# Up projections of two gated FFNs as Strassen block products, between the halves of the gate projection

## Chip, cores and metric

The kernel runs on one core of a Trainium2 chip, in one launch. The metric is the device time of one execution in microseconds. The core has a matrix engine (TensorE, PE in the profile; PEld is its loading of weights), a vector engine (VectorE, DVE), an engine for activation functions and scaled copies (ScalarE, ACT), a general one (GpSimd, POOL) and one that issues most of the DMAs (SyncE, SP).

## What is computed

Two layers over 512 tokens of 1024 features, fp32. Each layer is a mixer and a gated FFN, both after an RMS norm and both added to the residual; a last RMS norm follows. The change concerns the FFNs, the same in both layers, with 2816 hidden features:

```python
def gated_conv_ffn(x, w_gate, w_up, conv_w, conv_b, w_down):
    g = jnp.einsum('bsd,df->bsf', x, w_gate)
    g = causal_dwconv3(g, conv_w) + conv_b
    up = jnp.einsum('bsd,df->bsf', x, w_up)
    return jnp.einsum('bsf,fd->bsd', jax.nn.silu(g) * up, w_down)
...
    hn = rms_norm(h, norm_ffn[layer])
    h = h + gated_conv_ffn(hn, w_ffn_gate[layer], w_ffn_up[layer], conv_ffn[layer],
                           b_conv_ffn[layer], w_ffn_down[layer])
return rms_norm(h, final_norm)
```

`causal_dwconv3` is a convolution of three taps along the tokens, for each feature by itself.

## The kernel before

**Layout.** Activations lie transposed: features on the 128 partitions, the 512 tokens along the columns. The residual is eight tiles `h[k]`. An FFN's 2816 hidden features are 22 tiles of 128, taken in pairs f, f+1.

**Precision.** Each fp32 operand is held as two parts: a high part, rounded to the matrix engine's format by a copy on ScalarE, and a low part, the rest, by a subtraction on VectorE. One product of two operands is then three matmuls into the same bank, high by high, high by low, low by high (`mm3`, L126 to L128). Weights come from HBM by SyncE's queue into `raw` (four buffers of 512 KB, `fetch`), and `parts` makes `whi` (L121, ScalarE) and `wlo` (L122, VectorE), five buffers each. The split activations are `hgh` and `hgl`.

**Norm.** `Norm.add` multiplies a finished tile of h by the norm's gain, splits it into `hg[k]`, and sums its squares into `ssq`. The division by the norm is left for later: `rstd` adds `ssq` over the partitions by two matmuls with ones (L184, L185) and makes 1/sqrt on ScalarE and VectorE (L201 to L211), once the first pair's gates are done. Where a per-token column is wanted instead, L193 does it with one-column matmuls.

**An FFN.** `gate_up` handles one pair: two gate tiles and two up tiles, four banks of 512 columns, eight k tiles, three matmuls each: 96 matmuls of 512 columns. As each gate bank ends, VectorE evicts it times rstd into a padded row buffer (L465), three taps of the convolution follow on VectorE (L231 to L233), silu on ScalarE (L469), and GpSimd multiplies by rstd (L470), which is the up tile's norm. As each up bank ends, VectorE multiplies it with that (L474) and `split` makes the activation's two parts (L221, L223). After six pairs (and again after the other five; `HALVES`) the down projection adds into h, in layer 0 by `project` (weights against activations, two groups of four banks), in layer 1 by `group8` with eight banks, tokens on partitions. In layer 1 the residual is transposed into `y` by `turn_residual` during pairs 2 to 8.

**Order.** Instructions go to each engine's queue in an order that the Tile framework fixes when the program is built, and each queue is worked off in order. An instruction waits until its operands are there and its buffer is free; the number of buffers of a tag (`bufs`) limits how far an engine runs ahead. Seven banks of PSUM belong to matmul groups, one to small things.

Of the kernel before, what the change touches and what calls it, by code (L numbers as in the profile page):

```python
# [8 lines left out]
F32 = mybir.dt.float32  # L9
# [21 lines left out]
def tile_trunk(ctx: ExitStack, tc: tile.TileContext, x, norm_mix, norm_ffn, final_norm,  # L31
# [85 lines left out]

    def parts(raw, a, b, name):
        hi = wp.tile([P, a, b], F32R, tag="whi", bufs=5, name=f"whi_{name}")
        lo = wp.tile([P, a, b], F32R, tag="wlo", bufs=5, name=f"wlo_{name}")  # L120
        nc.scalar.activation(hi, raw, AF.Copy)  # L121
        nc.vector.tensor_tensor(lo, raw, hi.bitcast(F32), ALU.subtract)  # L122
        return hi, lo
# [6 lines left out]
    def group(name, outs, ks, lhs, rhs, tail, on_done, before=None):  # L130
# [6 lines left out]
        for i, j in order:  # L137
# [6 lines left out]
            if i == len(ks) - 1:  # L144
                on_done(j, banks[j])


    h = [cp.tile([P, S], F32, name=f"h{k}") for k in range(NK)]
# [6 lines left out]
    class Norm:  # L155
# [22 lines left out]
        def rstd(self):  # L178
            ps = aux_bank(f"ss_{self.name}")
            hi = tp.tile([P, S], F32R, tag=f"ms{S}", bufs=1, name=f"ssh_{self.name}")  # L180
            lo = tp.tile([P, S], F32R, tag=f"sd{S}", bufs=1, name=f"ssl_{self.name}")
# [14 lines left out]

    def newton(ms, n, name, r):


        sd = tp.tile([P, max(n, LINE)], F32, tag=f"sd{max(n, LINE)}", bufs=1, name=f"sd_{name}")[:, :n]  # L200
# [5 lines left out]
    def inv_sqrt(r, ss, n, name):  # L206

        ms = tp.tile([P, max(n, LINE)], F32, tag=f"ms{max(n, LINE)}", bufs=1, name=f"ms_{name}")[:, :n]
# [226 lines left out]
    HALVES = ((0, 12), (12, 22))  # L435

    def gate_up(layer, prm, rstd, ap, acts, f, tail):

        cs = slice(f * P, (f + 2) * P)
        ch = {}  # L440
        for half in range(2):
            for key, w in (("g", w_ffn_gate), ("u", w_ffn_up)) if tail < NK else ():
                ch[key, half] = weights(w[layer][half * 512 : (half + 1) * 512, cs]
                                        .rearrange("(k p) c -> p k c", p=P), 4, 256,
                                        f"{key}{layer}_{f}_{half}")
        if tail == NK:
            for key, w in (("g", w_ffn_gate), ("u", w_ffn_up)):
                for half in range(2):
                    ch[key, half] = weights(w[layer][half * 512 : (half + 1) * 512, cs]
                                            .rearrange("(k p) c -> p k c", p=P), 4, 256,  # L450
                                            f"{key}{layer}_{f}_{half}")

        def lhs(k, j):
            hi, lo = ch["gu"[j // 2], k // 4]
            c = slice((j % 2) * P, (j % 2 + 1) * P)
            return hi[:, k % 4, c], lo[:, k % 4, c]

        gates = {}

        def done(j, ps):  # L460
            ft = f + j % 2
            r = rstd()
            if j < 2:
                t = padded_tile()
                nc.vector.tensor_tensor(t[:, 2:], ps, r, ALU.mult)  # L465
# [3 lines left out]
                nc.scalar.activation(s, c, AF.Silu, bias=prm("bf", ft))  # L469
                nc.gpsimd.tensor_tensor(s, s, r, ALU.mult)  # L470
                gates[j] = s
            else:
                s = gates[j - 2]
                nc.vector.tensor_tensor(s, ps, s, ALU.mult)  # L474
                acts[ft] = split(ap, s, f"a{layer}_{ft}", tag="a", bufs=12)

        group(f"gu{layer}_{f}", range(4), list(range(NK)), lhs, lambda k, j: hg_k(k), tail, done)

    def lazy_rstd(norm):
        got = []  # L480

        def get():
            if not got:
                got.append(norm.rstd())
            return got[0]

        return get

    def ffn0(norm):
        nonlocal prm1  # L490
        with tc.tile_pool(name="f0", bufs=1) as ap:
            rstd = lazy_rstd(norm)
            nxt = None
            for a, b in HALVES:
                acts = {}
                for f in range(a, b, 2):
                    gate_up(0, prm0, rstd, ap, acts, f, 4 if f == 0 else NK)
# [3 lines left out]
                project(f"d0_{a}", w_ffn_down[0], acts, list(range(a, b)), nxt)  # L501
# [127 lines left out]
    def ffn1(norm):  # L629
        with tc.tile_pool(name="f1", bufs=1) as ap:  # L630
            fin = ap.tile([P, D], F32, name="fin")
            nc.scalar.dma_start(fin, final_norm.rearrange("(o d) -> o d", o=1).to_broadcast([P, D]))
            rstd = lazy_rstd(norm)
# [3 lines left out]
            def turn_residual(t):  # L637
                for half in range(2):
                    ps = mm_bank(f"hT{t}_{half}")
                    for i in range(4):  # L640
                        nc.tensor.transpose(ps[:, i * P : (i + 1) * P],
                                            h[half * 4 + i][:, t * P : (t + 1) * P], ident)
                    nc.scalar.copy(y[t][:, half * 512 : (half + 1) * 512], ps)
# [100 lines left out]
```

## Time and profile before

| | before |
|---|---|
| median of 3 runs | 1023.85 us (1020.9 to 1025.29) |
| profiled execution, its own time | 1023.1 us |
| span of its profile | 1021.4 us |
| mean granted TensorE clock | 0.998 |
| PE busy, matmuls | 1009.4 us, 99% |
| PEld busy | 832.4 us, 81% |
| DVE busy | 559.0 us, 55% |
| ACT busy | 345.3 us, 34% |
| POOL busy | 126.7 us, 12% |
| DMA | 101.24 MB, 99 GB/s on the mean |

Busy times are sums over the engine's instructions. PE and PEld run side by side, so their shares don't add up. The span is the time from the first instruction to the last in the profile; the execution's own time is 1.7 us longer. In the groups of the profile, `gu<-hgh,whi_g` is an FFN matmul into a gate or up bank from the high part of h and the high part of a gate weight; `128*128 128x512` is its weight tile and its moving tile.

### The profile page before, as it was taken

What the parts mean: (1) busy time and instruction counts of PE and PEld (TensorE: products, weight loads), DVE (VectorE), ACT (ScalarE), POOL (GpSimd) and SP (SyncE); (2) the same over time, 40 slices, a digit from 0 to 9 for tenths busy, and PEclk for the clock granted to TensorE, in tenths of its full rate; (3) what the DMA queues carried; (4) which work ended last, traced back from release to release, by engine and by line L of the source; (5) the groups of instructions that cost most, each with busy time, mean ns of one, the idle gap of its engine ahead of it and who ended that gap; (6) DMA issues with size and microseconds to landing.
All of it is one profiled execution on the core that took longest, in us unless ns stands there. A gap on an engine that the chain in (4) does not pass through costs nothing.

```text
span 1021.4 us, 11177 instructions
## 1 busy us (share of the span) xinstructions
PE 1009.4 (99%) x4485; PEld 832.4 (81%) x4485; DVE 559.0 (55%) x706; ACT 345.3 (34%) x449; POOL 126.7 (12%) x113
## 2 busy tenths in 40 slices
PE   9999999999999999999999999999999999999997
PEld 6788888888888888888878888888888888888885
DVE  5997567755623455654423645486554226565526
ACT  5423443323312223333345444433332212332313
POOL 3141121111100011111110001211111001111100
PEclk9999999999999999999999999999999999999999
DMA  7432233332333332332333123324233224233302
GB/s 232 154 103 83 83 103 98 92 115 89 95 111 84 96 109 83 103 104 78 106 126 103 62 91 96 103 83 124 83 103 103 84 81 124 83 104 103 100 3 83
DMA packets 74719, 101.24 MB, mean 99 GB/s; under 512 B 3268, under 2 KB 52652, under 8 KB 74668
## 3 DMA queue, kind: packets, MB, share of 16 engines
q1 hardware_dynamic: 73324, 98.96, 31.2%
q10 hardware_dynamic: 1344, 1.58, 0.5%
q8 instruction: 35, 0.57, 0.2%
q14 instruction: 16, 0.13, 0.0%
HBM read 98.42 MB, written 2.10 MB: 98 GB/s over the span
## 4 chain that ended last, share of the span: by engine, by line
PE 97%; DVE 1%; DMA 1%; issue 0%; POOL 0%; ACT 0%; DVEq 0%; POOLq 0%; ACTq 0%
PE gu L127 16%; PE gu L128 16%; PE gu L126 16%; PE dn L127 4%; PE d L126 4%; PE d L128 4%; PE dn L128 4%; PE d L127 4%; PE dn L126 4%; PE oo L128 1%; PE u L127 1%; PE u L126 1%; PE oo L127 1%; PE u L128 1%; PE oe L127 1%; PE oe L126 1%
## 5 line engine op out<-in xcount | busy, mean ns | idle before, releaser
L126 PE MATMUL gu<-hgh,whi_g 128*128 128x512 f32 x352 | 137.3, 390 | 0.0
L128 PE MATMUL gu<-hgh,wlo_g 128*128 128x512 f32 x352 | 137.0, 389 | 0.0
L128 PE MATMUL gu<-hgh,wlo_u 128*128 128x512 f32 x352 | 137.0, 389 | 0.0
L127 PE MATMUL gu<-hgl,whi_g 128*128 128x512 f32 x352 | 136.9, 389 | 0.0
L126 PE MATMUL gu<-hgh,whi_u 128*128 128x512 f32 x352 | 136.9, 389 | 0.0
L127 PE MATMUL gu<-hgl,whi_u 128*128 128x512 f32 x352 | 136.9, 389 | 0.0
L470 POOL TENSOR_TENSOR s<-s,rstd_f 128x512 f32<-128x512 f32 x44 | 66.5, 1512 | 529.8 <-ACT s L469 529.8
L121 ACT ACTIVATE whi_g<-raw_g 128x1024 fp32r<-128x1024 f32 x44 | 46.6, 1059 | 169.9 <-PE gu L127 107.8
L122 DVE TENSOR_TENSOR wlo_u<-raw_u,whi_u 128x1024 fp32r<-128x1024 f32 x52 | 63.8, 1229 | 59.5 <-ACT whi_u L121 59.1
L122 DVE TENSOR_TENSOR wlo_g<-raw_g,whi_g 128x1024 fp32r<-128x1024 f32 x44 | 54.4, 1236 | 47.3 <-ACT whi_g L121 46.9
L126 PEld LDWEIGHTS gu<-hgh,whi_u 128*128 128x128 f32 x352 | 66.1, 188 | 13.8
L127 PEld LDWEIGHTS gu<-hgl,whi_u 128*128 128x128 f32 x352 | 66.1, 188 | 13.7
L128 PEld LDWEIGHTS gu<-hgh,wlo_g 128*128 128x128 f32 x352 | 66.1, 188 | 13.7
L126 PEld LDWEIGHTS gu<-hgh,whi_g 128*128 128x128 f32 x352 | 66.1, 188 | 13.6
L128 PEld LDWEIGHTS gu<-hgh,wlo_u 128*128 128x128 f32 x352 | 66.1, 188 | 13.6
L127 PEld LDWEIGHTS gu<-hgl,whi_g 128*128 128x128 f32 x352 | 66.1, 188 | 13.6
L121 ACT ACTIVATE whi_u<-raw_u 128x1024 fp32r<-128x1024 f32 x52 | 55.0, 1059 | 58.6 <-PE gu L127 20.7
L126 PE MATMUL d<-a_hi,whi_d 128*128 128x512 f32 x176 | 68.6, 390 | 0.0
L128 PE MATMUL d<-a_hi,wlo_d 128*128 128x512 f32 x176 | 68.5, 389 | 0.0
L127 PE MATMUL d<-a_lo,whi_d 128*128 128x512 f32 x176 | 68.5, 389 | 0.0
L126 PE MATMUL dn<-whi_dn,a_hi 128*128 128x512 f32 x176 | 68.5, 389 | 0.0
L127 PE MATMUL dn<-wlo_dn,a_hi 128*128 128x512 f32 x176 | 68.5, 389 | 0.0
(236 smaller groups left out, 1772.5 us busy)
## 6 DMA issues: line engine op xcount, KB each, us to landing
raw_g<-in_w_ffn_gate_dram SPq DMA_DIRECT2D x44, 512.0 KB
raw_u<-in_w_ffn_up_dram SPq DMA_DIRECT2D x44, 512.0 KB, 3.9
raw_d<-in_w_ffn_down_dram SPq DMA_DIRECT2D x22, 512.0 KB, 3.5
raw_dn<-in_w_ffn_down_dram SPq DMA_DIRECT2D x22, 512.0 KB, 3.3
raw_oe<-in_w_out_even_dram SPq DMA_DIRECT2D x8, 512.0 KB, 3.3
raw_v<-in_w_in_odd_dram SPq DMA_DIRECT2D x8, 512.0 KB, 3.6
raw_u<-in_w_in_odd_dram SPq DMA_DIRECT2D x8, 512.0 KB, 3.5
raw_oo<-in_w_out_odd_dram SPq DMA_DIRECT2D x8, 512.0 KB, 3.3
```

The source lines that it names most:

```text
L121: nc.scalar.activation(hi, raw, AF.Copy)
L122: nc.vector.tensor_tensor(lo, raw, hi.bitcast(F32), ALU.subtract)
L126: nc.tensor.matmul(ps, lhs[0], rhs[0], start=start, stop=False)
L127: nc.tensor.matmul(ps, lhs[0], rhs[1], start=False, stop=False)
L128: nc.tensor.matmul(ps, lhs[1], rhs[0], start=False, stop=stop)
L470: nc.gpsimd.tensor_tensor(s, s, r, ALU.mult)
```

## The change

Of the 11 pairs of an FFN the first two (f = 0 and 2) stay as they were, now in `Ffn.direct`. The other nine (`Ffn.seven`) compute the two up tiles as a product of 2 by 2 blocks. With A the two weight tiles against the two halves of the contraction, and B the normalized activations, the two halves of the contraction against the two halves of the tokens, it makes

- sums of weights S1 = A21+A22, S2 = S1-A11, S3 = A11-A21, S4 = A12-S2 (tiles `s14`, `s23`),
- sums of activations T1 = B12-B11, T3 = B22-B12, T2 = T3+B11, T4 = B21-T2 (tiles `t41`, `t23`), once in an FFN,
- seven block products P1 = A11 B11, P2 = A12 B21, P3 = S4 B22, P4 = A22 T4, P5 = S1 T1, P6 = S2 T2, P7 = S3 T3, each twelve matmuls (four k pairs, three parts) of 256 columns,
- the four blocks of the result P1+P2, P1+P6+P5+P3, P1+P6+P7+P4, P1+P6+P7+P5. P1, P6, P7 and P4 are accumulated in one bank, with copies of the bank kept between them.

So 48 matmuls of 512 columns become 84 of 256. On TensorE the order in such a pair is P1, the first half of the gates' k tiles, P6, the second half, P7, P5, P2, P4, P3.

What goes with it:

- The sums need activations that are normalized in full. During pair 2, `normalize` multiplies two h tiles at a time by gain and rstd, splits them into `hg` again, makes their four sums and splits those. In pairs from 4 on the gates are evicted without rstd, by a copy on ScalarE, and GpSimd's multiplication is gone.
- The first tap of the convolution moves from VectorE to ScalarE.
- In those pairs the gate weights' low part is no longer made by VectorE: `summed` copies the raw weights times -1 to `lo` on ScalarE, and a DMA issued from GpSimd's queue adds `raw` to it; `hi` is a second copy on ScalarE. (The copy to `lo` rounds to the matrix engine's format, so the sum is the rest that the subtraction gave.)
- The activations are projected down in four parts of an FFN (`PARTS`) instead of two, and `a` has 6 buffers instead of 12.
- In layer 1 the T2, T3 tiles take the buffers of the residual tiles h, so `turn_residual` moves into pair 0's loop over k, and pair 0's tail, the last k tiles that each bank goes through by itself, is two k tiles instead of four. The final norm's gain is loaded late, into a `raw` buffer. Some small tiles share buffers (`pk`, and the norm's work tiles in `sq`).

The diff, cut to its core (in the changed kernel the matmul of `multiply` is line 621, those of `mm3` are L135 to L137):

```diff
-        pk = cp.tile([P, P], F32, tag=f"pk{layer}", name=f"pk{layer}")
+        pk = cp.tile([P, P], F32, tag="pk", bufs=1, name=f"pk{layer}")
...
+    def summed(raw, a, b, name):
+
+        hi = wp.tile([P, a, b], F32R, tag="whi", bufs=5, name=f"whi_{name}")
+        lo = wp.tile([P, a, b], F32R, tag="wlo", bufs=5, name=f"wlo_{name}")
+        nc.scalar.activation(lo, raw, AF.Copy, scale=-1.0)
+        nc.gpsimd.dma_start(lo, raw, accum_op=ALU.add)
+        nc.scalar.activation(hi, raw, AF.Copy)
+        return hi, lo
...
-    HALVES = ((0, 12), (12, 22))
-
-    def gate_up(layer, prm, rstd, ap, acts, f, tail):
...
+    PARTS = ((0, 6), (6, 12), (12, 18), (18, 22))
+    HALF = S // 2
+    NP = NK // 2
+    PAIRS = [k for i in range(NP) for k in (i, i + NP)]
...
+        def conv(self, t, ft):
+            ap, prm, n = self.ap, self.prm, f"{self.layer}_{ft}"
+            c = ap.tile([P, S], F32, tag="c", bufs=2, name=f"c{n}")
+            nc.scalar.activation(c, t[:, 0:S], AF.Copy, scale=prm("cf", ft))
+            for i in (1, 2):
+                nc.vector.scalar_tensor_tensor(c, t[:, i : S + i], prm("cf", i * NF + ft), c,
+                                               op0=ALU.mult, op1=ALU.add)
+            return c
+
+        def silu(self, c, ft):
+            s = self.ap.tile([P, S], F32, tag="s", bufs=3, name=f"s{self.layer}_{ft}")
+            nc.scalar.activation(s, c, AF.Silu, bias=self.prm("bf", ft))
+            return s
+
+        def act(self, ft, s):
+            self.acts[ft] = split(self.ap, s, f"a{self.layer}_{ft}", tag="a", bufs=6)
+
+        def direct(self, f, ks, tail, before=None, at_end=None):
+            layer = self.layer
...
+            gates = {}
+
+            def done(j, ps):
+                ft = f + j % 2
+                r = self.rstd()
+                if j < 2:
+                    t = padded_tile()
+                    nc.vector.tensor_tensor(t[:, 2:], ps, r, ALU.mult)
+                    s = self.silu(self.conv(t, ft), ft)
+                    nc.gpsimd.tensor_tensor(s, s, r, ALU.mult)
+                    gates[j] = s
+                else:
+                    s = gates[j - 2]
+                    nc.vector.tensor_tensor(s, ps, s, ALU.mult)
+                    self.act(ft, s)
+
+            group(f"gu{layer}_{f}", range(4), ks, lhs, lambda k, j: hg_k(k), tail, done,
+                  before, at_end)
+
+        def normalize(self, kp):
+
+            n, r = f"{self.layer}_{kp}", self.rstd()
+            x = self.ap.tile([P, 2, S], F32, tag="sum", bufs=2, name=f"x{n}")
+            for i, k in enumerate((kp, kp + NP)):
+                nc.vector.scalar_tensor_tensor(x[:, i, :], h[k], self.prm("ffn", k), r,
+                                               op0=ALU.mult, op1=ALU.mult)
+
+            def halves(dst, src):
+                nc.scalar.activation(dst[0], src, AF.Copy)
+                nc.vector.tensor_tensor(dst[1], src, dst[0].bitcast(F32), ALU.subtract)
+
+            halves(hg[kp], x[:, 0, :])
+            halves(hg[kp + NP], x[:, 1, :])
+            b11, b12 = x[:, 0, :HALF], x[:, 0, HALF:]
+            b21, b22 = x[:, 1, :HALF], x[:, 1, HALF:]
+            t = self.ap.tile([P, 4, HALF], F32, tag="sum", bufs=2, name=f"t{n}")
+            nc.vector.tensor_tensor(t[:, 1, :], b22, b12, ALU.subtract)
+            nc.vector.tensor_tensor(t[:, 0, :], t[:, 1, :], b11, ALU.add)
+            nc.vector.tensor_tensor(t[:, 3, :], b12, b11, ALU.subtract)
+            nc.vector.tensor_tensor(t[:, 2, :], b21, t[:, 0, :], ALU.subtract)
+            self.t23[kp] = self.sums(kp)
+            halves(self.t23[kp], t[:, :2, :])
+            self.t41[kp] = self.ap.tile([P, 2, 2, HALF], F32R, name=f"t41_{n}")
+            halves((self.t41[kp][:, 0], self.t41[kp][:, 1]), t[:, 2:, :])
+
+        def moving(self, product, kp):
+
+            if product in (1, 2, 3):
+                k = kp if product == 1 else kp + NP
+                c = slice(HALF, S) if product == 3 else slice(0, HALF)
+                return hg[k][0][:, c], hg[k][1][:, c]
+            if product in (6, 7):
+                return tuple(t[:, product - 6, :] for t in self.t23[kp])
+            return tuple(self.t41[kp][:, n, {4: 0, 5: 1}[product], :] for n in range(2))
+
+        def seven(self, f):
+            layer, ap, n = self.layer, self.ap, f"{self.layer}_{f}"
+            raws = ffn_weights(layer, f, [(key, half) for key in "ug" for half in range(2)])
+            r0, r1 = raws["u", 0][0], raws["u", 1][0]
+            stat = {}
+
+            def pair(name):
+                return [wp.tile([P, 2, 4, P], F32R, tag=f"w{x}", bufs=5, name=f"w{x}_{name}_{n}")
+                        for x in ("hi", "lo")]
+
+            def halves(hi, lo, src):
+                nc.scalar.activation(hi, src, AF.Copy)
+                nc.vector.tensor_tensor(lo, src, hi.bitcast(F32), ALU.subtract)
+
+            def put(product, hi_lo, i):
+                stat[product] = hi_lo[0][:, i], hi_lo[1][:, i]
+
+            w = pair("a11")
+            halves(w[0][:, 0], w[1][:, 0], r0[:, :, :P])
+            put(1, w, 0)
+            gate = [summed(*raws["g", 0])]
+            s23 = ap.tile([P, 2, 4, P], F32, tag="sum", bufs=2, name=f"s23_{n}")
+            s14 = ap.tile([P, 2, 4, P], F32, tag="sum", bufs=2, name=f"s14_{n}")
+            nc.vector.tensor_tensor(s14[:, 0], r0[:, :, P:], r1[:, :, P:], ALU.add)
+            nc.vector.tensor_tensor(s23[:, 0], s14[:, 0], r0[:, :, :P], ALU.subtract)
+            nc.vector.tensor_tensor(s23[:, 1], r0[:, :, :P], r0[:, :, P:], ALU.subtract)
+            w = pair("s23")
+            halves(*w, s23)
+            put(6, w, 0)
+            put(7, w, 1)
+            gate.append(summed(*raws["g", 1]))
+            nc.vector.tensor_tensor(s14[:, 1], r1[:, :, :P], s23[:, 0], ALU.subtract)
+            w = pair("s14")
+            halves(*w, s14)
+            put(5, w, 0)
+            put(3, w, 1)
+            hi, lo = parts(*raws["u", 1])
+            for i, product in enumerate((2, 4)):
+                c = slice(i * P, (i + 1) * P)
+                stat[product] = hi[:, :, c], lo[:, :, c]
+
+            BANK = {1: "a", 6: "a", 7: "a", 4: "a", 5: "e", 3: "e", 2: "b"}
+            banks, opened = {}, set()
+
+            def multiply(product):
+                at = BANK[product]
+                if at not in banks:
+                    banks[at] = mm_bank(f"u{at}{n}")
+                ps = banks[at][:, :HALF]
+                hi, lo = stat[product]
+                for kp in range(NP):
+                    b_hi, b_lo = self.moving(product, kp)
+                    a_hi, a_lo = hi[:, kp, :], lo[:, kp, :]
+                    for l, r, end in ((a_hi, b_hi, False), (a_hi, b_lo, False),
+                                      (a_lo, b_hi, kp == NP - 1)):
+                        nc.tensor.matmul(ps, l, r, start=at not in opened, stop=end,
+                                         skip_group_check=True)
+                        opened.add(at)
+                return ps
+
+            def gates(half):
+                for k in PAIRS[half * 4 : half * 4 + 4]:
+                    for j in range(2):
+                        if j not in banks:
+                            banks[j] = mm_bank(f"g{j}{n}")
+                        hi, lo = gate[k // 4]
+                        c = slice(j * P, (j + 1) * P)
+                        mm3(banks[j], (hi[:, k % 4, c], lo[:, k % 4, c]), hg_k(k),
+                            k == PAIRS[0], k == PAIRS[-1])
+
+            kept = ap.tile([P, 3, HALF], F32, tag="kept", bufs=2, name=f"kept{n}")
+
+            def keep(i, ps):
+                nc.scalar.copy(kept[:, i, :], ps)
+
+            def add(i, ps):
+                nc.vector.tensor_tensor(kept[:, i, :], ps, kept[:, i, :], ALU.add)
+
+            keep(0, multiply(1))
+            gates(0)
+            keep(1, multiply(6))
+            gates(1)
+            c, s = [], []
+            for j in range(2):
                 t = padded_tile()
-                nc.vector.tensor_tensor(t[:, 2:], ps, r, ALU.mult)
-                c = ap.tile([P, S], F32, tag="c", bufs=2, name=f"c{layer}_{ft}")
-                conv3(c, t, *(prm("cf", i * NF + ft) for i in range(3)))
-                s = ap.tile([P, S], F32, tag="s", bufs=3, name=f"s{layer}_{ft}")
-                nc.scalar.activation(s, c, AF.Silu, bias=prm("bf", ft))
-                nc.gpsimd.tensor_tensor(s, s, r, ALU.mult)
-                gates[j] = s
+                nc.scalar.copy(t[:, 2:], banks[j])
+                c.append(self.conv(t, f + j))
+            keep(2, multiply(7))
+            for j in range(2):
+                s.append(self.silu(c[j], f + j))
+            ps = multiply(5)
+            p2 = multiply(2)
+            add(2, ps)
+            add(0, p2)
+            ps = multiply(4)
+            nc.vector.tensor_tensor(s[1][:, HALF:], kept[:, 2, :], s[1][:, HALF:], ALU.mult)
+            nc.vector.tensor_tensor(s[1][:, :HALF], ps, s[1][:, :HALF], ALU.mult)
+            self.act(f + 1, s[1])
+            add(1, multiply(3))
+            s0 = s[0].rearrange("p (a b) -> p a b", a=2)
+            nc.vector.tensor_tensor(s0, kept[:, :2, :], s0, ALU.mult)
+            self.act(f, s[0])
+
+        def hidden(self, f, arrival=None, before=None):
+            if f == 0:
+                self.direct(f, arrival or list(range(NK)), 2 if before else 4, before)
+            elif f == 2:
+                def ready(k):
+                    i = PAIRS.index(k)
+                    if i in (2, 4, 6):
+                        self.normalize(i // 2 - 1)
+
+                self.direct(f, PAIRS, 1, ready, lambda: self.normalize(NP - 1))
             else:
-                s = gates[j - 2]
-                nc.vector.tensor_tensor(s, ps, s, ALU.mult)
-                acts[ft] = split(ap, s, f"a{layer}_{ft}", tag="a", bufs=12)
-
-        group(f"gu{layer}_{f}", range(4), list(range(NK)), lhs, lambda k, j: hg_k(k), tail, done)
-
-    def lazy_rstd(norm):
-        got = []
-
-        def get():
-            if not got:
-                got.append(norm.rstd())
-            return got[0]
-
-        return get
+                self.seven(f)
...
+            def sums(kp):
+                return [cp.tile([P, 2, HALF], F32R, tag=f"h{k}", name=f"t23_{k}")
+                        for k in (kp, kp + NP)]
+
+            ffn = Ffn(1, prm1, norm, ap, sums)
+            acts = ffn.acts
...
+            def before(k):
+                if 1 <= k <= 4:
+                    turn_residual(k - 1, 0)
+                elif k > 4:
+                    turn_residual(k - 5, 1)
+
+            for a, b in PARTS:
                 for f in range(a, b, 2):
-                    gate_up(1, prm1, rstd, ap, acts, f, 4 if f == 0 else NK)
-                    if 2 <= f <= 8:
-                        turn_residual((f - 2) // 2)
+                    ffn.hidden(f, before=before if f == 0 else None)
+                    if f == 0:
+                        turn_residual(3, 1)
                 last = b == NF
                 if last:
+                    fin = wp.tile([P, D], F32, tag="raw", bufs=4, name="fin")
+                    nc.scalar.dma_start(
+                        fin, final_norm.rearrange("(o d) -> o d", o=1).to_broadcast([P, D]))
```

More of the change, by code (lines that the diff above doesn't have):

```diff
@@ L143, in group @@
             mm3(banks[j], lhs(ks[i], j), rhs(ks[i], j), i == 0, i == len(ks) - 1)
-            if i == len(ks) - 1:
+            if i == len(ks) - 1 and at_end is None:
                 on_done(j, banks[j])
-    h = [cp.tile([P, S], F32, name=f"h{k}") for k in range(NK)]
+        if at_end is not None:
+            at_end()
+            for j in outs:
+                on_done(j, banks[j])
+    h = [cp.tile([P, S], F32, tag=f"h{k}", name=f"h{k}") for k in range(NK)]
     hg = [(cp.tile([P, S], F32R, name=f"hgh{k}"), cp.tile([P, S], F32R, name=f"hgl{k}"))
@@ L491, in ffn0 @@
         with tc.tile_pool(name="f0", bufs=1) as ap:
[L492 removed]
+            def sums(kp):
+                return [ap.tile([P, 2, HALF], F32R, name=f"t23{i}_{kp}") for i in "hl"]
+            ffn = Ffn(0, prm0, norm, ap, sums)
             nxt = None
[L494 to L495 removed]
+            for a, b in PARTS:
                 for f in range(a, b, 2):
[L497 removed]
+                    ffn.hidden(f)
                 if b == NF:
```

77 lines of the change are left out of this document (38 added, 39 removed).

## Prediction

> **What bounds the kernel now.** I read the page first (busy shares, the chain that ended last), then the costliest groups.
>
> ```profile
> span 1021.4 us, 11177 instructions
> PE 1009.4 (99%) x4485; PEld 832.4 (81%) x4485; DVE 559.0 (55%) x706; ACT 345.3 (34%) x449; POOL 126.7 (12%) x113
> ...
> PE 97%; DVE 1%; DMA 1%; issue 0%; POOL 0%; ACT 0%; DVEq 0%; POOLq 0%; ACTq 0%
> ```
>
> TensorE is busy for 99% of the span and 97% of the chain lies on it, so only two things move the time: fewer or shorter products, or holes between them. VectorE looks half idle, but that is a mean over stages. The record of a product is longer than the distance between two, so the price of a product is read from starts, in the timeline of TensorE:
>
> ```profile
> 663.73 0.39 PE L128 MATMUL gu<-hgh,wlo_g 128*128 128x512 f32 x1
> 663.96 0.39 PE L126 MATMUL gu<-hgh,whi_g 128*128 128x512 f32 x1
> 664.19 0.39 PE L127 MATMUL gu<-hgl,whi_g 128*128 128x512 f32 x1
> 664.41 0.39 PE L128 MATMUL gu<-hgh,wlo_g 128*128 128x512 f32 x1
> ```
>
> Three steps in 0.68 us: 0.227 us for a 512-column product. A pair of FFN columns (96 products) is 21.8 us.
>
> **Fewer columns, narrower products.** In 18 of the 22 pairs, 48 up products of 512 columns (10.9 us) become 84 of 256. No such product is in this trace. From below it is half of 0.227, 0.113. Each still loads its own 128 columns of weights; what such loads cost when nothing hides them is seen at L193, whose products have one column (weight loads, then one row of TensorE):
>
> ```profile
> 527.79 1.08 PEld L193 LDWEIGHTS ssc_m<-small,ssq_m 128*128 128x128 f32 x8
> 528.79 0.19 PEld L126 LDWEIGHTS v<-whi_v,hgh 128*128 128x128 f32 x1
> 528.91 0.19 PEld L127 LDWEIGHTS v<-wlo_v,hgh 128*128 128x128 f32 x1
> ...
> 528.01 0.95 PE L193 MATMUL ssc_m<-small,ssq_m 128*128 128x1 f32 x8
> ```
>
> The first of the eight products starts at 528.01, and at 528.91 the loads have gone through seven more of L193 and one of L126: 8 in 0.90 us, 0.112 each. Load and stream are equally long, so neither hides much of the other. I take 0.12, a little above both rows; the upper end is the length of a load's record, 0.19. At 0.12 the 84 cost 10.1 us: 0.8 us saved in a pair, 18 pairs: **14 us gained** (24 at 0.113; none above 0.13).
>
> **Normalizing, which is new.** The block products need an activation that is already divided by its norm, so in each FFN, during pair 2, VectorE multiplies all eight h tiles by rstd, splits them again, and builds four sums for each of four pairs of tiles. Pair 4 waits for this. In the built program VectorE's queue holds 65 instructions from the end of rstd to the low part of the first weight sums (s23), which TensorE's second block product reads. Their prices, by form:
>
> ```profile
> L122 DVE TENSOR_TENSOR wlo_u<-raw_u,whi_u 128x1024 fp32r<-128x1024 f32 x52 | 63.8, 1229 | 59.5 <-ACT whi_u L121 59.1
> L121 ACT ACTIVATE whi_g<-raw_g 128x1024 fp32r<-128x1024 f32 x44 | 46.6, 1059 | 169.9 <-PE gu L127 107.8 <-PE dn L128 23.0 <-issue 19.4
> L232 DVE SCALAR_TENSOR_TENSOR c<-rows,prm,c 128x512 f32<-128x512 f32 x44 | 33.6, 768 | 0.7
> L223 DVE TENSOR_TENSOR a_lo<-s,a_hi 128x512 fp32r<-128x512 f32 x44 | 31.6, 718 | 14.1 <-ACT a_hi L221 14.1
> L469 ACT ACTIVATE s<-c,prm 128x512 f32<-128x512 f32 x44 | 31.4, 718 | 70.9 <-DVE c L233 70.9
> L474 DVE TENSOR_TENSOR s<-gu,s 128x512 f32<-128x512 f32 x44 | 30.3, 690 | 44.6 <-PE gu L128 43.3 <-PE prm_ps L94 0.7 <-POOL s L470 0.6
> L465 DVE TENSOR_TENSOR rows<-gu,rstd_f 128x512 f32<-128x512 f32 x44 | 30.2, 691 | 60.8 <-PE gu L128 60.7
> L643 ACT COPY y<-hT 128x512 f32<-128x512 f32 x8 | 4.6, 572 | 0.0
> ```
>
> VectorE: 4 evictions with rstd (L465) 2.8; 8 products h by gain by rstd and 8 conv taps (both as L232) 12.3; 16 low parts (as L223) 11.5; 16 sums of 256 columns, which the slope from 690 ns at 512 to 1229 at 1024 puts at 0.42 each, 6.7; 4 gated products (L474) 2.8; 3 low parts of activations 2.2; five 512-wide operations on weights 3.5; one 1024-wide low part 1.2. Sum **43 us**. When it can begin is seen in VectorE's timeline, with the product that releases it (a row of the tile view: first and last start):
>
> ```profile
> L185 PE MATMUL ss_f<-ssl_f,ones_r x2: 389/389/389, 161.8 to 664.9; 128*128 128x512 f32 x2
> ...
> 162.24 0.69 DVE L209 TENSOR_SCALAR ms_f<-ss_f 128x512 f32<-128x512 f32 x1 [1.08 <-PE ss_f L185]
> 163.62 3.35 DVE L202 RECIPROCAL rstd_f<-sd_f 128x512 f32<-128x512 f32 x1 [0.70 <-ACT sd_f L201]
> 166.89 1.16 DVE L122 TENSOR_TENSOR wlo_u<-raw_u,whi_u 128x1024 fp32r<-128x1024 f32 x1
> 169.41 0.69 DVE L211 SCALAR_TENSOR_TENSOR rstd_f<-ms_f,rstd_f 128x512 f32<-128x512 f32 x1
> 170.14 1.29 DVE L465 TENSOR_TENSOR rows<-gu,rstd_f 128x512 f32<-128x512 f32 x2
> ```
>
> rstd is usable 8.3 us after the product at 161.8; 36 products of pair 0 follow that one (8.2 us), so pair 2 starts as rstd is ready, at 170.1. From there TensorE has pair 2 (21.8), the first block product (12 by 0.12, 1.4), six gate products (1.4) and six more that its queue puts before s23's low part (1.1): 25.7 us. VectorE's list ends at 43: **17 us of hole** in layer 0. The rest of VectorE's present load does not go away by itself:
>
> ```profile
> core 0: us, PE busy (x) PEld busy (x) DVE busy (x) ACT busy (x) POOL busy (x), PEclk, DMA share, GB/s
> 170.10:191.90 21.80, 21.80 (x98) 18.06 (x97) 19.47 (x27) 9.83 (x12) 6.89 (x4) 1.00 0.31 92
> 191.90:213.60 21.70, 21.70 (x97) 17.96 (x97) 12.76 (x16) 6.80 (x8) 3.01 (x2) 1.00 0.33 97
> ```
>
> In pair 2 VectorE is busy for 19.5 of 21.8 us already, against 12.8 in the pair after: the place chosen for normalizing is the fullest of the FFN. In layer 1 the change also shortens pair 0's tail to two tiles and puts the residual's transposes into its loop: only 18 products (4.1 us) follow the norm's, and one 512-wide low part stands ahead of rstd's end, so rstd comes some 4.7 us into pair 2: **21 us**. At the far end, if all of it were hidden, zero; no reason makes it a gain.
>
> **The gates' low parts by DMA.** VectorE's subtraction (1.23 us, 36 times) becomes a negated copy on ScalarE and an adding DMA from GpSimd's queue, SBUF to SBUF, 512 KB. None is in this trace. The nearest are the weight loads:
>
> ```profile
> q1 hardware_dynamic: 73324, 98.96, 31.2%
> ...
> raw_u<-in_w_ffn_up_dram SPq DMA_DIRECT2D x44, 512.0 KB, 3.9
> raw_dn<-in_w_ffn_down_dram SPq DMA_DIRECT2D x22, 512.0 KB, 3.3
> out_dram<-y SPq DMA_DIRECT2D x8, 256.0 KB, 2.1
> ```
>
> A plain 512 KB lands in 3.3 to 3.9 us. The queue's share (31.2% of 1021 us for 98.96 MB) gives 1.7 us of all 16 engines for 512 KB; an addition must also read its destination, so I add that once to 3.6: 5.2 us. The lower bound is 2.1 (a smaller store), the upper, with GpSimd writing the descriptors, about 8 (two plain landings in a row).
>
> What hides it: the buffer of the second gate half's low part comes free only after the previous pair's fourth block product, and ScalarE's queue reaches its negated copy after eleven instructions that follow the previous gate's end: copies of two banks (0.57 each) and of one half bank (0.36), two first taps and two silus (0.72 each), four 1024-wide (1.06 each), 8.6 us, begun 0.4 before that end, so 8.2. TensorE meanwhile has six block products (72 by 0.12) and nine gate products, 10.7 us. Cover 2.5, so a DMA of 5.2 makes a **wait of 2.7 in each of ten pairs** that follow another such pair, and everything behind it in TensorE's queue waits. In the six that follow a down projection the buffer is freed 1.4 us before the projection's end, ScalarE is done 0.7 after it, TensorE has 4.1 us of work: cover 3.4, **wait 1.8**. In pair 4, after the normalizing hole, 2.6 more, twice. The first gate half's copy is made 3.6 us earlier and is covered.
>
> The Trainium skill, "DMA: Bandwidth & Descriptors", section "Anatomy of one DMA", gives a GpSimd-issued DMA 2.0 us plus bytes by 436 GB/s, an estimate of 3.2 us here, below the trace's own 3.3 to 3.9 for plain loads; by it the sum would be some 36 us lower. No run here shows which holds for an adding one.
>
> **At nothing.** GpSimd's scaling of gates (L470) goes; it hung off ScalarE and nobody waited. In a block pair VectorE has 14.4 us of work and ScalarE 14.4 by the rows above, in about 21: neither binds. Four down projections instead of two add h and y additions on VectorE, behind products of the next pair. Queues of SP hold the same loads; their buffers now come free by a DMA's landing, more than 6 us before they are needed.
>
> **After a hole the clock.** After short work and an idle stretch early in the kernel, products stood further apart:
>
> ```profile
> 9.23 0.63 PE L127 MATMUL z<-hgl,whi_z 128*128 128x512 f32 x1
> 9.65 0.50 PE L128 MATMUL z<-hgh,wlo_z 128*128 128x512 f32 x1
> 9.99 0.39 PE L127 MATMUL z<-hgl,whi_z 128*128 128x512 f32 x1
> 10.22 0.40 PE L128 MATMUL z<-hgh,wlo_z 128*128 128x512 f32 x1
> ```
>
> 0.42 apart at first, 0.23 from 9.99 on. After each normalizing hole I charge some seven products at the slow rate, 1.5 us: 3 us. "TensorE: Matmul & The Clock Gate" of the Trainium skill (Part 1) says that an idle window of about 3.4 us halves the clock until a busy one has passed; the trace's 0.42 against 0.23 agrees with the halving.
>
> **Sum**, against the profiled execution's own 1023.1 us: -14 + 17 + 21 + 5 (pair 4's waits) + 27 (ten by 2.7) + 11 (six by 1.8) + 3 = +70, so 1093. The median of the runs lies 0.75 above that execution: **1094 us**.
>
> **Rivals.**
> *The DMA is hidden.* If it lands within 3.3 us, as the fastest plain load does, the ten waits are 0.8, the six none, pair 4's two 0.7 each: 1023.8 - 14 + 38 + 8 + 1 + 3 = 1060; at 2.1 us 1051. For it: the data never leave SBUF. Against it: twice the reads.
> *The DMA is slow.* At 8 us every wait grows by 2.8, 18 times: 1144, and holes of over 5 us could bring the slow clock into each pair.
> *Faster.* The products are the only bound, because VectorE's list fits under TensorE: it decides at 26 us where I count 43, so its operations would have to take 0.6 of their price, and the DMA at most 2.5. Then 1023.8 - 14 = 1010, or 1000 at 0.113 a product. Every row above speaks against it; a partial case turns faster when the two holes and all waits together stay under 14 us.
> *Narrow products bound by loading*, 0.19 instead of 0.12: about 700 of them stand outside the stretches that wait anyway: +49, 1143. The 0.112 row speaks against it.
>
> **How the numbers follow.** Forecast (DMA between 3.5 and 7 us, holes near 17 and 21) 0.66; DMA hidden 0.12; DMA slow 0.15; faster 0.05; narrow products 0.02. The low end takes in the hidden DMA at its lower bound, 1050; the upper the slow one to nearly its bound, 1140. Within 0.5% (about what a measurement can tell from no change) is a sliver between the faster rival and the rest, 0.02, taken from the forecast's lower tail; slower 0.93.
>
> **What would show it.** Right: TensorE idle for 15 to 22 us once in each FFN, ended by VectorE's wlo_s23; VectorE near 100% in the 40 us after rstd; L621's products 0.12 apart; in the other block pairs TensorE idle before L137 of the gates, released by the adding DMA. Wrong: no hole after pair 2, or a DMA landing under 2.5 us, or L621 spaced 0.19.

## The result, and the profile after

The changed kernel takes **1088.8 us** (median of 4 runs, 1088.3 to 1093.9) against 1023.0 of the kernel before on the same chip: 1.065 times as long, with a 95% interval of 1.061 to 1.069. The forecast was 1094, slower. Its profiled execution took 1088.84 us, with a span of 1087.1: 65.7 more than before.

From the page of the changed kernel (busy us, share of the span, instructions; then the queues with packets, MB and their share of 16 DMA engines):

```profile
span 1087.1 us, 12945 instructions
PE 1014.5 (93%) x5133; PEld 855.7 (79%) x5133; DVE 623.4 (57%) x882; ACT 479.8 (44%) x687; POOL 106.0 (10%) x113
...
PEclk9999999699999999999999999996999999999999
...
q0 software_dynamic: 5184, 18.88, 10.0%
```

TensorE was idle for 12.0 us of its span before (1021.4 less 1009.4); now it is for 72.6 (1087.1 less 1014.5), and two slices have a lower clock, the places behind pair 2 of each layer. The view of waits says what ended the idle time; its columns are us in total, times, longest:

```profile
engine line waited for: us in total, times, longest us
PE g L137 <- DMA wlo_g<-raw_g: 33.3, 24, 2.0
PE ua L621 <- ACT whi_s L577: 9.8, 1, 9.8
PE ua L621 <- POOL s L520: 8.4, 1, 8.4
PE ua L621 <- ACT hgh L539: 7.1, 3, 3.8
PE ua L621 <- DVE wlo_s L578: 1.7, 1, 1.7
```

The first row is the adding DMA's waits, many and short (two of them, 2.7 us, lie inside the holes). The others are the two holes. Together they are 60.3 us, nearly all of the 60.6 us by which TensorE's idle time grew.

**The products.** TensorE's timeline in a block pair (start, length, engine, line):

```profile
286.28 0.28 PE L621 MATMUL ua<-hgh,whi_a 128*128 128x256 f32 x1
286.40 0.28 PE L621 MATMUL ua<-hgl,whi_a 128*128 128x256 f32 x1
286.52 0.28 PE L621 MATMUL ua<-hgh,wlo_a 128*128 128x256 f32 x1
```

The starts are 0.12 apart, which was the forecast's value between its bounds of 0.113 and 0.19.

**The hole behind pair 2 in layer 0**, from the timelines of VectorE, ScalarE and TensorE:

```profile
168.45 0.69 DVE L229 SCALAR_TENSOR_TENSOR rstd_f<-ms_f,rstd_f 128x512 f32<-128x512 f32 x1
205.06 0.68 DVE L591 TENSOR_TENSOR s<-raw_u 128x512 f32<-128x512 f32 x1
205.78 1.05 ACT L577 ACTIVATE whi_s<-s 128x1024 fp32r<-128x1024 f32 x1
206.93 0.55 PE L621 MATMUL ua<-t23h,whi_s 128*128 128x256 f32 x1 [8.37 <-POOL s L520]
208.53 1.21 DVE L578 TENSOR_TENSOR wlo_s<-s,whi_s 128x1024 fp32r<-128x1024 f32 x1
```

rstd is done at 169.14, VectorE's list ends with `wlo_s` at 209.74, 40.6 us later. TensorE goes on when ScalarE has `whi_s` (206.83), made from the sums that VectorE finished just before. In the program this product waits for `whi_s`, not for the instruction of GpSimd that the row names, which ended at about the same moment. The windows show the same stretch (us; busy with instruction counts; then clock, DMA share, GB/s):

```profile
core 0: us, PE busy (x) PEld busy (x) DVE busy (x) ACT busy (x) POOL busy (x), PEclk, DMA share, GB/s
170.10:191.90 21.80, 21.80 (x102) 18.22 (x101) 20.02 (x38) 13.40 (x20) 3.61 (x2) 1.00 0.01 2
192.00:206.90 14.90, 3.27 (x12) 1.63 (x11) 14.90 (x24) 8.09 (x14) 4.57 (x3) 0.66 0.32 71
206.90:213.60 6.70, 6.54 (x24) 5.46 (x25) 5.99 (x8) 4.71 (x6) 0.88 (x1) 0.50 0.49 128
```

In the 14.9 us after pair 2 and the first block product of pair 4 VectorE is busy without a gap and TensorE for 3.3 us. For another 6.7 us TensorE works at half its clock.

In layer 1 TensorE stood at this place for `whi_s` and, two products later, for `wlo_s` as well:

```profile
744.49 0.80 PE L621 MATMUL ua<-t,whi_s 128*128 128x256 f32 x2 [9.77 <-ACT whi_s L577]
746.98 0.58 PE L621 MATMUL ua<-t,wlo_s 128*128 128x256 f32 x1 [1.70 <-DVE wlo_s L578]
```

**One wait for an adding DMA**: ScalarE's, GpSimd's and TensorE's timelines between pairs 8 and 10 of layer 0, and what the tile view says of this DMA's landing:

```profile
277.89 0.59 ACT L651 COPY rows<-g 128x512 f32<-128x512 f32 x1 [0.23 <-PE g L137]
281.32 1.05 ACT L122 ACTIVATE wlo_g<-raw_g 128x1024 fp32r<-128x1024 f32 x1
284.44 1.05 ACT L122 ACTIVATE wlo_g<-raw_g 128x1024 fp32r<-128x1024 f32 x1
282.67 0.85 POOL L123 DMA_DIRECT2D wlo_g<-raw_g  x1 [17.91 <-ACT wlo_g L122]
285.79 0.85 POOL L123 DMA_DIRECT2D wlo_g<-raw_g  x1 [2.27 <-DVE s L661]
288.53 0.50 PE L137 MATMUL g<-hgh,wlo_g 128*128 128x512 f32 x1 [0.90 <-DMA wlo_g<-raw_g]
291.01 0.50 PE L137 MATMUL g<-hgh,wlo_g 128*128 128x512 f32 x1 [0.61 <-DMA wlo_g<-raw_g]
...
DMA to landing us min/median/max: 4.5/4.6/5.8
```

The second copy ends at 285.49, 7.6 us after the eviction of the previous pair's gate began. The DMA is issued at 285.79 and lands 5.2 us later (the tile view of this one alone); TensorE goes on at 291.01. The last row is over all 36 DMAs. TensorE stood for the first half's low part too.

### The profile page after: what moved, and what is told of

It reads as the page before. It is cut to its first block, busy times and chain, and to the rows that moved or that the text cites. A ratio compares the mean times of both kernels' runs of the same rounds, so it can differ in the third digit from the quotient of the medians.

```text
span 1087.1 us, 12945 instructions
## 1 busy us (share of the span) xinstructions
PE 1014.5 (93%) x5133; PEld 855.7 (79%) x5133; DVE 623.4 (57%) x882; ACT 479.8 (44%) x687; POOL 106.0 (10%) x113
## 5 line engine op out<-in xcount | busy, mean ns | idle before, releaser
L137 PE MATMUL g<-hgh,wlo_g 128*128 128x512 f32 x288 | 114.2, 406 | 33.6 <-DMA wlo_g<-raw_g 33.3
L135 PE MATMUL g<-hgh,whi_g 128*128 128x512 f32 x288 | 114.6, 398 | 0.1
L136 PE MATMUL g<-hgl,whi_g 128*128 128x512 f32 x288 | 114.2, 397 | 0.0
L137 PEld LDWEIGHTS g<-hgh,wlo_g 128*128 128x128 f32 x288 | 53.7, 191 | 53.2 <-DMA wlo_g<-raw_g 42.8
L489 DVE SCALAR_TENSOR_TENSOR c<-rows,prm,c 128x512 f32<-128x512 f32 x88 | 64.6, 758 | 17.8 <-ACT c L487 17.3
L135 PE MATMUL dn<-whi_dn,a_hi 128*128 128x512 f32 x176 | 68.6, 390 | 0.0
L137 PE MATMUL dn<-whi_dn,a_lo 128*128 128x512 f32 x176 | 68.5, 389 | 0.0
L137 PE MATMUL d<-a_hi,wlo_d 128*128 128x512 f32 x176 | 68.5, 389 | 0.0
L135 PE MATMUL d<-a_hi,whi_d 128*128 128x512 f32 x176 | 68.2, 390 | 0.0
L135 PEld LDWEIGHTS g<-hgh,whi_g 128*128 128x128 f32 x288 | 55.2, 192 | 11.0 <-ACT whi_g L124 0.4
L136 PEld LDWEIGHTS g<-hgl,whi_g 128*128 128x128 f32 x288 | 55.3, 192 | 10.3
L122 ACT ACTIVATE wlo_g<-raw_g 128x1024 fp32r<-128x1024 f32 x36 | 37.8, 1050 | 56.6 <-PE dn L136 56.6
L578 DVE TENSOR_TENSOR wlo_s<-s,whi_s 128x1024 fp32r<-128x1024 f32 x36 | 44.1, 1224 | 32.0 <-ACT whi_s L577 31.9
```

What stands on the lines that cost most here:

```text
L122: nc.scalar.activation(lo, raw, AF.Copy, scale=-1.0)
L135: nc.tensor.matmul(ps, lhs[0], rhs[0], start=start, stop=False)
L136: nc.tensor.matmul(ps, lhs[0], rhs[1], start=False, stop=False)
L137: nc.tensor.matmul(ps, lhs[1], rhs[0], start=False, stop=stop)
L489: nc.vector.scalar_tensor_tensor(c, t[:, i : S + i], prm("cf", i * NF + ft), c, op0=ALU.mult, op1=ALU.add)
L578: nc.vector.tensor_tensor(lo, src, hi.bitcast(F32), ALU.subtract)
```

## The experiments

Theory: two independent losses, the adding DMA (about 37 us, since its chain starts late) and VectorE's list in front of pair 4 (about 33 us and some slow clock), against a gain of 14 by narrower work. Rivals: the waits belong to ScalarE's queue or to buffers, whoever makes the low parts; VectorE has no room for the subtractions; the DMAs cost by their bytes; the block products don't gain. The kernel before was measured beside them again: 1021.6 us with the first four, 1022.6 with the last three, 1023.0 above. Differences between times of different sections are good to about 1 us.

### The DMA replaced by the subtraction

```diff
-            gate = [summed(*raws["g", 0])]
+            gate = [parts(*raws["g", 0])]
...
-            gate.append(summed(*raws["g", 1]))
+            gate.append(parts(*raws["g", 1]))
```

> The changed kernel with the gate weights' low parts made by VectorE's subtraction again, no adding DMA. Theory (TensorE's 33 us of waits for low parts of gates are the adding DMA's 4.6 us behind ScalarE's copy): they go, so does the slow-clock stretch that one of them brings (2 us); VectorE's list in the two holes grows by two subtractions at most, 2 us each. 1089 - 33 - 2 + 4 = 1058, from 1050 to 1062. Rival A (the wait is for ScalarE's queue or for the buffer, whoever makes the low part): the 1.2 us subtraction comes behind the same copies, the waits shrink to a third at most: 1078 or more. Rival B (VectorE has no room for 36 subtractions more): new waits for wlo_s, 1075 or more.

Measured: 1050.4 us, 38.4 less than the changed kernel; ratio to before 1.028 (1.026 to 1.029). Its waits:

```profile
PE ua L621 <- issue: 10.5, 1, 10.5
PE ua L621 <- ACT whi_s L577: 8.1, 1, 8.1
PE ua L621 <- ACT hgh L539: 8.1, 3, 4.7
PE g L137 <- DVE wlo_g L131: 3.2, 1, 3.2
```

All are in the two holes (the first row, named "issue", is layer 0's, ended at 209.14 just after ScalarE had `whi_s`). Between block pairs nothing of note is left, though the low parts still come from behind ScalarE's copies. So rival A falls: what costs is the way through the DMA, 4.5 to 5.8 us to its landing, where the subtraction takes 1.2. (The edit also takes ScalarE's negated copy away, 1.05 us each; this run doesn't price that apart.) Rival B falls too. The time was at the expectation's lower end.

### The block sums moved a pair later

Pair 4 is computed by 96 plain products from the normalized activations; `normalize` in pair 2 stops after splitting x into `hg`, and a function called during pair 4 makes x once more and then the sums.

```diff
             halves(hg[kp], x[:, 0, :])
             halves(hg[kp + NP], x[:, 1, :])
+
+        def block_sums(self, kp):
+            x = ...   # h by gain by rstd once more; then t23 and t41 as they were
...
+            elif f == 4:
+                self.direct(f, PAIRS, 1, then, normed=True)   # then: block_sums after each pair of k
```

> The changed kernel, adding DMA kept, with pair 4 computed by 96 plain products from the normalized activations, and the block sums built during pair 4 instead of pair 2 (they multiply h by gain and rstd once more). Theory (the two holes after pair 2 are VectorE's list, as long as it is, against TensorE's work): before pair 4's last low parts of weights VectorE has some 29 us to do instead of 41, and TensorE comes to them 27 us after rstd in layer 0, 23 in layer 1: holes of about 2 and 7 us instead of 13 and 18, and the slow clock after them mostly goes (6 us). Two block pairs fewer cost 1.6, two pairs' waits for the DMA go (2). 1089 - 22 - 6 + 2 - 2 = 1061, from 1055 to 1070. Rival (the hole is the chain of ScalarE and VectorE through hgh, or a buffer that pair 2 holds): it stays, 1085 or more.

Measured: 1061.6 us, 27.2 less; ratio to before 1.038 (1.036 to 1.040). Its waits:

```profile
PE g L137 <- DMA wlo_g<-raw_g: 30.3, 19, 2.6
PE gu L137 <- DVE wlo_u L131: 2.5, 3, 1.4
PE gu L137 <- DVE wlo_g L131: 2.3, 2, 1.9
```

The holes are down to a few us, and the DMA's waits are untouched but for the three that lay in pair 4 (33.3 less 3.1). So the holes were VectorE's list: they went when the list was shortened ahead of pair 4's weights.

### Both

The two edits together.

> Both edits together: low parts of the gates by subtraction, block sums during pair 4. If the two losses are independent, 1061 - 33 = 1028, from 1018 to 1035, about the kernel before. If VectorE is short of time once both are on it: 1040 or more.

Measured: 1019.4 us, ratio to before 0.9975 (0.9965 to 0.9985). The two edits save 38.4 and 27.2 alone, together 69.4 (the sum would be 65.6): the losses are independent within 4 us, and the 66 us by which the change was slower are gone. The gain of the block products is not yet seen whole: the kernel is 2 us below the kernel before, where 16 block pairs are worth some 11 ("No block products", below). The same edits without block products take 8 us more than the kernel before, so that much of the rest of the change, with its normalizing, still costs.

### The adding DMA alone in the kernel before

```diff
-                    ch[key, half] = weights(w[layer][half * 512 : (half + 1) * 512, cs]
+                    raw = fetch(w[layer][half * 512 : (half + 1) * 512, cs]
...
+                    ch[key, half] = summed(*raw) if key == "g" and f >= 4 else parts(*raw)
```

> The kernel before with one part of the change alone: the gate weights' low parts in the pairs from f = 4 on by ScalarE's negated copy and the adding DMA. Theory (it is the place that costs, a chain started late): here the buffer of a gate half's low part is free by the middle of the previous pair, 10.9 us ahead, copy and DMA take about 7, so it is covered; behind the down projections some waits of 2 to 3 us: 1023 to 1032. Rival (the transfers themselves cost: 18.9 MB more past the weight loads, late weights): 1040 or more.

Measured: 1023.0 us, ratio 1.001 (1.000 to 1.002). One wait row of it, and the landing from the tile view:

```profile
PE gu L136 <- DMA wlo_g<-raw_g: 0.6, 1, 0.6
...
DMA to landing us min/median/max: 4.5/4.8/8.2
```

The same 36 copies and DMAs, landing no sooner, cost about 1 us here, where they can start with half a pair of products and more still to come: in layer 0 the 18 low parts landed 11 to 15 us before TensorE used them. Not their bytes cost, but the place that the change gives them.

### Each adding DMA in two halves

```diff
-        nc.gpsimd.dma_start(lo, raw, accum_op=ALU.add)
+        for q in range(0, a, 2):
+            nc.gpsimd.dma_start(lo[:, q : q + 2], raw[:, q : q + 2], accum_op=ALU.add)
```

> The changed kernel with each adding DMA cut in two of 256 KB, by k tiles; TensorE's first use needs only the first. Theory (size sets the 4.6 us: the queue's share, 10.0% of 1087 us for 36 of them, is 3.0 us of all 16 engines each): the first half lands some 1.5 us sooner, in each of some 21 waits: 1089 - 26 = 1063, from 1055 to 1075. Rival (a fixed latency is most of it): the first half lands no sooner, 1085 to 1095.

Measured: 1068.0 us, 20.8 less than the changed kernel, where 26 was expected; ratio to before 1.044 (1.043 to 1.046).

```profile
PE g L138 <- DMA wlo_g<-raw_g: 16.3, 22, 2.5
...
DMA to landing us min/median/max: 3.3/4.3/8.4
```

The waits halve. The quickest landing falls from 4.5 to 3.3 us for half the size: an estimate from these two is 1.2 us for 256 KB and 2.1 whatever the size. So size and fixed part both count, and neither theory holds alone. The Trainium skill, "DMA: Bandwidth & Descriptors", section "Anatomy of one DMA", has 2.0 us fixed, which agrees; an estimate by its 436 GB/s is 0.6 us for 256 KB, which an adding DMA here doubles.

### No block products

The kernel with subtraction and later sums, and every pair from f = 4 on by 96 plain products; the sums of activations are still built, unused.

```diff
             else:
-                self.seven(f)
+                self.direct(f, PAIRS, 4, normed=True)
```

> The kernel with subtraction and later sums, but every pair from f = 4 on computed as pair 4: 96 plain products, no block products; the sums of activations are still built and go unused. Theory (a block pair is worth 0.8 us, 84 products 0.120 apart against 48 of 0.227): 16 pairs, 1019.4 + 12.8 = 1032, from 1029 to 1036. Rival (narrow products cost more elsewhere, or block pairs bring hidden waits): 1026 or less.

Measured: 1030.3 us; ratio to before 1.008 (1.007 to 1.010), against 0.9975 with the block products. That is 11 us for 16 pairs, 0.69 each, give or take 0.12. The gain is there, a little under the 0.82 that the distances give (48 by 0.2267 less 84 by 0.1198). Whole pairs in the two traces agree with it: successive block pairs start 20.99 to 21.07 us apart in the kernel with subtraction and later sums, plain pairs 21.76 apart here, 0.75 less on the mean.

### The norm earlier

The kernel with subtraction and later sums, with `rstd`'s two matmuls put into pair 0 in front of its fourth k tile:

```diff
+                def first(k):
+                    if k == 3:
+                        self.rstd()
+                    if before:
+                        before(k)
...
-                self.direct(f, arrival or list(range(NK)), 2 if before else 4, before)
+                self.direct(f, arrival or list(range(NK)), 2 if before else 4, first)
```

> The kernel with subtraction and later sums, and the two matmuls with ones for rstd put after 36 of pair 0's products instead of behind its first gate bank (60 in layer 0, 78 in layer 1). Theory (what is left of the holes is VectorE's list, begun at rstd): rstd comes 5.4 and 9.5 us earlier, VectorE does the norm's chain while it has little else, the holes of 2.9 and 5.7 us go: 1019.4 - 8 = 1011, from 1010 to 1016. Rival (the sum of squares is not ready by then, or the chain delays the low parts of pair 2's weights): TensorE waits in pair 0 or 2 instead, 1018 or more.

Measured: **1015.0 us** (1014.5 to 1015.5); ratio to before 0.993 (0.992 to 0.994). Its waits in the FFNs:

```profile
PE gu L137 <- DVE wlo_u L131: 1.2, 2, 0.6
PE dn L135 <- DVE s L528: 1.0, 1, 1.0
PE d L135 <- ACT a_hi L239: 0.8, 1, 0.8
```

What was left of the holes is nearly gone: 4.4 us gained of the 8 expected, since a last wait for `wlo_u` stays and a new one of 1.0 for a down projection's activations comes. This version beats both kernels, the kernel before by 0.7%.

## Why the prediction was right

The sign, the size (+65.7 in the span, +70 forecast) and all three mechanisms were as forecast: holes behind pair 2 by VectorE's list, waits for the adding DMA, a small gain by the narrower products. Single terms were off by up to 5 us and partly cancelled, so it is in part luck that the total came so near. What each measured is worked out from the distances between starts of successive products, less 0.227 or 0.120 (a record runs on into a wait, so the view of waits shows some 0.2 us less for each); the first row is from whole pairs:

| step | forecast | measured |
|---|---|---|
| narrower products, 18 pairs | -14 | -13.4 at 0.75 a pair; -12.4 at 0.69 |
| holes, layers 0 and 1 | 17 + 21 | 13.0 + 20.3 |
| slow clock | 3 | 8.4 |
| DMA, pair 4 | 5 | 0.5 |
| DMA, ten pairs | 27 | 21.6 |
| DMA, six pairs behind a down projection | 11 | 15.2 |

With the first of the two values for the products the measured terms come to 65.6. A wait that ends inside a hole with the landing of an adding DMA (1.6 us in layer 0, 1.5 in layer 1) is counted with the hole, since VectorE's list went on behind it.

- **Products.** 0.12 was right. In block pairs some products of 512 columns stand 0.231 to 0.236 apart instead of 0.227 (0.228 on the mean), which takes the pair's gain from 0.82 to 0.75; the 0.69 of the run without block products agrees with that within its 0.12.
- **Holes.** VectorE's list of 65 in layer 0 took 40.6 us, not 43, and that is near by luck. The forecast added up the lengths of records, but a record of 0.69 starts 0.60 after the one before (186.31, 186.91, 187.51), which makes the list some 6 us shorter; 1.8 us of waits for GpSimd and 2.1 us more for two instructions of 1.75 us beside GpSimd's multiplications (why they take longer is not shown) were not in the forecast. In layer 0 TensorE stood for the high part of s23, not for the low part as the forecast said: its queue holds products of the gates that don't need the adding DMA in front of the low part's, and the low part was there as they ended. So the list counted only up to 206.83, 37.7 us after rstd. The 24.8 us of work that TensorE had from there were close to the forecast's 25.7. The hole of 13.0 lies under the 15 to 22 that the forecast named as its sign. In layer 1 the low part did end the hole, as forecast, and its 20.3 are close to the 21.
- **Slow clock.** Seven products at the slow rate were charged for each hole. The window above shows 6.7 us at half the clock in layer 0; they cost 3.6 us. In layer 1 the slow clock cost 3.1 us behind the hole, and once more 1.7 behind a wait of only 2.0 us.
- **DMA.** The ten pairs were too dear by half a us each, but not by the DMA. There the second half's DMA lands 4.8 to 5.5 us after its issue, 5.3 as a rule, and 5.2 was charged. By itself an adding DMA mostly lands in 4.5 to 4.7 us; those issued while the first half's is still under way take 4.8 to 5.8. The forecast had no row of an adding DMA, so it is in part luck that its 5.2 fits. The term that was mis-sized is what hides the DMA: ScalarE's eleven instructions took 7.6 us where their records add up to 8.6, since records overlap here too (behind a copy of 1.05 us at 385.55 the next starts at 386.50), and 0.3 us from the copy's end to the issue were left out. The first half's low part, which the forecast called covered, was waited for in two of the ten pairs by more than 0.3 us (0.90 above). In pair 4 the DMA landed inside the hole. Behind the down projections the forecast took both layers alike; layer 0 gave its 1.8 (measured 1.6 each), layer 1 some 3.4, because there the first half's copy waits for the end of the projection too (it holds the weights' buffers), and the second half's comes four instructions behind it, with a DMA that lands 5.7 us after its issue. ScalarE's and TensorE's timelines in layer 1:

```profile
798.41 1.06 ACT L122 ACTIVATE wlo_g<-raw_g 128x1024 fp32r<-128x1024 f32 x1 [18.86 <-PE dn L136]
802.22 1.04 ACT L122 ACTIVATE wlo_g<-raw_g 128x1024 fp32r<-128x1024 f32 x1
804.30 0.73 PE L137 MATMUL g<-hgh,wlo_g 128*128 128x512 f32 x2 [1.30 <-DMA wlo_g<-raw_g]
809.34 0.73 PE L137 MATMUL g<-hgh,wlo_g 128*128 128x512 f32 x2 [1.59 <-DMA wlo_g<-raw_g]
```

- **The rivals.** The Trainium skill's "DMA: Bandwidth & Descriptors", section "Anatomy of one DMA", gave the estimate of 3.2 us for a DMA of this size; it was not borne out, 4.5 us is the least here. That VectorE's list fits under TensorE's work did not happen either, but the experiments show that it can be made to, all but some 3 us: then the kernel is 0.7% faster than before, half of the 14 us that the products promised.

## What to carry to other kernels

Fewer products are a gain only when the work that feeds them is in place: price a change on the matrix engine by the queue that must finish ahead of it, counted from the moment its input is there, and move what is not yet needed behind that point. Add up such a queue by the distances between starts, not by the lengths of records: on ScalarE and VectorE here these differ by some 0.1 us an instruction. The adding DMA in the place of the subtraction took some 4 us longer to be there; it cost about 1 us in all where its source and its buffer were ready half a pair ahead, and some 2 us in each pair where it started at the end of a chain. Two losses that don't share a place can be taken out one by one, and each alone tells its own price.

## What the hardware showed that was not expected

- After the hole in layer 0 the clock stayed at half for 6.7 us in which TensorE's records leave only 0.2 us free (the window from 206.9 to 213.6). "TensorE: Matmul & The Clock Gate" of the Trainium skill, Part 1, gives at least one busy window of about 3.4 us for the way back, in windows that run freely; 6.7 us is just under two, the far end of that.
- A wait of only 2.0 us (829.0 to 831.2 in layer 1) was followed by seven products at 0.43, while others of the same length were not. The traces show what sets them apart, though no run was made for it. The granted clock is down from 196.74 to 213.81, from 729.22 to 753.12 and from 831.62 to 835.04: these lengths, and the 78.5 us between the last two, are 5, 7, 1 and 23 times 3.41 us, so it changes on a fixed grid of stretches of that length. Two of them with such a wait, and between them the one behind the first:

```profile
core 0: us, PE busy (x) PEld busy (x) DVE busy (x) ACT busy (x) POOL busy (x), PEclk, DMA share, GB/s
828.21:831.62 3.41, 1.56 (x8) 1.08 (x7) 2.55 (x3) 1.28 (x3) 0.00 (x0) 1.00 0.99 204
831.62:835.04 3.42, 3.42 (x10) 2.64 (x9) 1.95 (x4) 0.00 (x0) 0.00 (x0) 0.50 0.87 264
852.10:855.52 3.42, 1.61 (x7) 0.97 (x6) 3.13 (x4) 2.12 (x4) 0.00 (x0) 1.00 1.04 193
```

Counted at 0.227 and 0.120 us each (twice that at half the clock), products fill 38% of the first, and the clock is halved for the next; they fill 42% of the last, and it is not halved behind it. Counted like this, in all traces of this case the clock fell in the FFNs behind every stretch filled to 38% or less, and behind none filled to 40% or more. It came back behind stretches filled to 80% or more, not behind 77% or less: the one from 206.98 to 210.40 was filled to 77%, and the slow clock of layer 0 went on until 213.81. By these counts it is where a wait of some 2 us lies in the grid that decides whether the slow clock comes on top of it.
- Adding 512 KB from SBUF to SBUF takes 4.5 us at the least, 256 KB 3.3.
